# Weights laid out as one run per partition, and two loads held behind x, in a hybrid decoder layer on eight cores

## Chip, cores, metric

One Trainium2 chip, all 8 cores, one program on each. The time is the device time of the slowest core in microseconds (us). Most executions agree within 0.3%. Some fall into a slower state, in which the cores of one or both dies run longer; they are left out of every ratio.

## The reference, cut to what matters

One decoder layer on 8192 tokens of width 2048, causal, f32. Each core takes 1024 tokens and a halo of 128 (1152 columns, `TM`). All weights are read by every core.

```python
h = rms_norm(x, g_pre_mix) * (1.0 + scale_m) + shift_m     # mod = silu(c) @ w_ada + b_ada
u, v, p, ga, gb = split(h @ w_in)                          # 9216 columns
y_a = spatial_gating(gelu(u), gelu(v), ...) @ w_branch_a
y_b = multiscale_pool(p, ...) @ w_branch_b
mix = (sigmoid(ga) * y_a + sigmoid(gb) * y_b) @ w_out
x = x + gate_m * rms_norm(mix, g_post_mix)                 # "first/second norm pass" below
h = rms_norm(x, g_pre_ffn) * (1.0 + scale_f) + shift_f
a, g = split(causal_depthwise_conv(h @ w_up))
x = x + gate_f * rms_norm((gelu(a) * g) @ w_down, g_post_ffn)
```

## The kernel before

A small recording layer (`Sched`) collects every operation with what it reads and writes, orders the operations of each engine by a simulated clock, and puts in the semaphore waits. Hence one line of the source (L296, L303, L330 and so on) stands for all matmuls, all activations or all transfers; the tile names tell them apart. Activations lie feature-major (128 features on the partitions, tokens along the row). Weights are f32 in HBM and are cast to bf16 by the transfer, which GpSimd issues. They go to a ring of three slots (`RING`); x and the output are moved by transfers that SyncE issues.

```python
def load(key, where, w, r0, nk, c0, ncols, parts=1, only=None, after=()):
    dst = piece_dst(where, nk, ncols)
    n = nk // parts
    for i in range(parts) if only is None else only:
        d = dst[:, i * n:(i + 1) * n, :]
        src = w[(r0 + i * n) * 128:(r0 + (i + 1) * n) * 128, c0:c0 + ncols].rearrange("(k p) n -> p k n", p=128)
        last = S.dma("pool", d, src, writes=[d])
```

A slot is 16 k-blocks (kc) by 512 columns: each partition gets 16 separate rows of 512 f32, 2 KB read and 1 KB landed. Pieces of `w_ada` have rows of 1536 or 2048 columns (6 or 8 KB read), but for sB, whose rows are 512. Pieces are named after what they hold: sA, sB, h, gm, sf, hf, gf are parts of `w_ada`; pA, v, u of `w_in`; o of `w_out`; up of `w_up`. kc 12 to 15 are the last four k-blocks of the normalised x; they need sB's scale.

The start, cut: `sA0` to `sA3` and `sB` are the parts of `w_ada` that give the first scale (12 of 16 blocks of features from the sA, four from sB), `pA` the first projection weights (`w_in`, in four transfers of four kc).

```python
load("sA0", 0, *specs["sA0"]);  load("sA1", 1, *specs["sA1"])
for kc in range(KC):
    S.dma("sp", xres[kc], xT[kc * 128:(kc + 1) * 128, :], writes=[xres[kc]])
...
for kc in range(6): x_stats(kc)          # square on ScalarE, sum by a matmul with ones
scale_mms("sA0", 0, 0, 12)
load("sA2", 0, *specs["sA2"])
for kc in range(6, 12): x_stats(kc)
scale_mms("sA1", 4, 0, 12)
load("sA3", 1, *specs["sA3"])
load("pA", 2, *specs["pA"], only=[0, 1, 2])
...                                      # rstd, x * rstd, then sA2, sB, pA[3], sA3, scale, h for kc 0 to 11
```

The first norm pass (642 columns, `PCS_1`), which adds x again, stores the sum, and takes the next mean square, beside output-projection matmuls:

```python
for i in range(16):
    m, x = mixT[:, i, c0:c0 + n], xs[i % len(xs)]
    S.dma("sp", x, xT[i * 128:(i + 1) * 128, 126 + c0:126 + c0 + n], writes=[x])
    S.tt(m, m, rs, ALU.mult)
    S.tt(m, m, x, ALU.add)
    S.act(sqx[i % 4][:, 0:n], m, AF.Square)
    sum_mms(b0, sqx[i % 4], pieces, i == 0, i == 15)
    S.dma("sp", outT[...], mixT[:, i, lo:c0 + n], ...)
```

`up000` is the first piece of `w_up`; GpSimd issues it when the ring slot of `o1` is free, which falls into this pass.

Of the kernel before, what the change touches and what calls it, by code (L numbers as in the profile page):

```python
# [14 lines left out]
D = 2048  # L15
# [22 lines left out]
class Sched:  # L38
# [5 lines left out]

    def __init__(self):
        self.ops = []
        self.mem = {}
        self.tags = {}
        self.names = list(self.ENGS) + ["d%s%d" % (e, i) for e, n in self.NDMA.items() for i in range(n)]
        self.classes = {"pe": 0, "pes": 1, "act": 2, "dve": 3, "pool": 4, "dma": 5}  # L50
# [161 lines left out]

    def emit(self, block, sems):
        seq = self.order()
        self.prods = {p: [] for p in self.names}
        q = {e: [] for e in self.ENGS}
        know = {e: {} for e in self.ENGS}
        next_dma = {e: 0 for e in self.NDMA}
        for o in seq:
            deps = {}  # L220
            if o.dma:
                i = next_dma[o.eng]
                next_dma[o.eng] = (i + 1) % self.NDMA[o.eng]
                o.prod, o.inc = "d%s%d" % (o.eng, i), 16
            else:
                o.prod, o.inc = o.eng, 1
            o.seq, o.signal, o.waits = len(self.prods[o.prod]), o.dma, []
            if o.dma and o.seq:
                deps[o.prod] = o.seq - 1
            for d in o.deps:  # L230
                d = self.ops[d]
                if d.eng == "pe" and o.eng == "pe":
                    continue
                if deps.get(d.prod, -1) < d.seq:
                    deps[d.prod] = d.seq
            k = know[o.eng]
            todo = [(p, s) for p, s in deps.items() if k.get(p, -1) < s]
            for p, s in list(todo):
                if any(self.prods[p2][s2].know.get(p, -1) >= s for p2, s2 in todo if (p2, s2) != (p, s)):
                    todo.remove((p, s))  # L240
            for p, s in todo:
                d = self.prods[p][s]
                d.signal = True
                o.waits.append((p, s))
                for p2, s2 in d.know.items():
                    if k.get(p2, -1) < s2:
                        k[p2] = s2
                if k.get(p, -1) < s:
                    k[p] = s
            o.know = dict(k)  # L250
            self.prods[o.prod].append(o)
            q[o.eng].append(o)
        self.q = q
        value = {}
        for p, lst in self.prods.items():
            n, vals = 0, []
            for o in lst:
                if o.signal:
                    n += o.inc
                vals.append(n)  # L260
            value[p] = vals

        def run(name, e):
            for o in q[name]:
                for p, s in o.waits:
                    e.wait_ge(sems[p], value[p][s])
                ins = o.fn(e)
                if o.signal:
                    ins.then_inc(sems[o.prod], o.inc)
            if name == "sp":  # L270
                for p, lst in self.prods.items():
                    if lst and p.startswith("d"):
                        e.wait_ge(sems[p], value[p][-1])

        block.tensor(lambda e: run("pe", e))
        block.scalar(lambda e: run("act", e))
        block.vector(lambda e: run("dve", e))
        block.gpsimd(lambda e: run("pool", e))
        block.sync(lambda e: run("sp", e))
# [51 lines left out]
                       after=after)  # L331


def build_program():
    nc = bass.Bass("TRN2", target_bir_lowering=False)

    def din(name, shape, dt=F32):
        return nc.dram_tensor(name, list(shape), dt, kind="ExternalInput").ap()

    xT = din("xT", [D, TM])  # L340
    c_col = din("c_col", [128, KC])
    w_ada = din("w_ada", [D, 6 * D])
    b_ada_fm = din("b_ada_fm", [128, 96])
    vec_fm_d = din("vec_fm", [128, NV])
    bs_exp_d = din("bs_exp", [1, 1024])
# [2 lines left out]
    wpool_d = din("wpool", [128, 4 * 2 * 256])  # L348
    hmask_d = din("hmask", [128, 1])
    pfix_d = din("pfix", [128, 64])  # L350
    w_in = din("w_in", [D, 9216])
    w_ba = din("w_branch_a", [D, D])
    w_bb = din("w_branch_b", [1024, D])
    w_out = din("w_out", [D, D])
    w_up = din("w_up", [D, 2 * FFN])
    w_down = din("w_down", [FFN, D])
    outT = nc.dram_tensor("outT", [D, TOK], F32, kind="ExternalOutput").ap()

    S = Sched()
# [1 line left out]
    with contextlib.ExitStack() as es:  # L361
# [40 lines left out]

        slot_queue = {}
        loaded = {}

        def piece_dst(where, nk, ncols):
            if isinstance(where, int):
                return v3(RING[:, where * 8192:where * 8192 + nk * ncols], nk)
            return view(where[0], where[1], nk * ncols * 2, BF16, nk)

        def load(key, where, w, r0, nk, c0, ncols, parts=1, only=None, after=()):
            dst = piece_dst(where, nk, ncols)
            n = nk // parts
            for i in range(parts) if only is None else only:
                d = dst[:, i * n:(i + 1) * n, :]
                src = w[(r0 + i * n) * 128:(r0 + (i + 1) * n) * 128, c0:c0 + ncols].rearrange("(k p) n -> p k n", p=128)
                last = S.dma("pool", d, src, writes=[d])
            loaded[key] = dst
            return last

        specs = {}
# [6 lines left out]
        def load_next(slot):  # L428
            if slot_queue.get(slot):
                key = slot_queue[slot].pop(0)  # L430
                load(key, slot, *specs[key])

        def bank(b):
            return ps[:, b * 512:(b + 1) * 512]
# [64 lines left out]

        def sec_specs(name, sec):  # L500
            for i in range(4):
                specs["%s%d" % (name, i)] = (w_ada, i * 4, 4, sec * D, D)

        for nm, sec in (("gm", 2), ("sf", 4), ("hf", 3), ("gf", 5)):
            sec_specs(nm, sec)
        for i in range(4):
            specs["sA%d" % i] = (w_ada, i * 4, 4, D, 1536)
        specs["sB"] = (w_ada, 0, KC, D + 1536, 512, 4)
        for i in range(8):
            specs["h%d" % i] = (w_ada, i * 2, 2, 0, D)  # L510
        specs["pA"] = (w_in, 0, KC, 4096 + 512, 512, 4)
        specs["pB"] = (w_in, 0, KC, 4096, 512)
        specs["bb0"] = (w_bb, 0, 8, 0, 1024)
        specs["bb1"] = (w_bb, 0, 8, 1024, 1024)
        for g in range(4):
            specs["u%d" % g] = (w_in, 0, KC, g * 512, 512)
            specs["v%d" % g] = (w_in, 0, KC, 2048 + g * 512, 512, 1 if g else 4)
            specs["ga%d" % g] = (w_in, 0, KC, 5120 + g * 512, 512)
            specs["gb%d" % g] = (w_in, 0, KC, 7168 + g * 512, 512)
            specs["ba%d" % g] = (w_ba, 0, KC, g * 512, 512)  # L520
            specs["o%d" % g] = (w_out, 0, KC, g * 512, 512)
        UPP = ((0, 512), (512, 512), (1024, 384))
        for k in range(NG):
            for half in range(2):
                for i, (c0, n) in enumerate(UPP):
                    specs["up%d%d%d" % (k, half, i)] = (w_up, 0, KC, half * FFN + k * GB * 128 + c0, n)
            for q in range(4):
                specs["dn%d%d" % (k, q)] = (w_down, k * GB, GB, q * 512, 512)

        run = ["v0", "gm0", "v1", "gm1", "v2", "gm2", "v3", "gm3", "u0", "u1", "u2", "u3"]  # L530
        mods = ["sf0", "sf1", "sf2", "sf3", "hf0", "hf1", "hf2", "hf3"]
# [42 lines left out]
        S.memset(vsum[:], 0.0)  # L574
        S.memset(vstat[:], 0.0)
        for kc in range(KC):
            S.dma("sp", xres[kc], xT[kc * 128:(kc + 1) * 128, :], writes=[xres[kc]])
            if kc == 7:
                for t, d in ((bada, b_ada_fm), (vec, vec_fm_d)):
                    S.dma("sp", t[:], d[:, :], writes=[t[:]])  # L580
# [13 lines left out]
        for kc in range(6):  # L594
            x_stats(kc)
        scale_mms("sA0", 0, 0, 12)
        load("sA2", 0, *specs["sA2"])
        for kc in range(6, 12):
            x_stats(kc)
        scale_mms("sA1", 4, 0, 12)  # L600
        load("sA3", 1, *specs["sA3"])
        load("pA", 2, *specs["pA"], only=[0, 1, 2])
        for kc in range(12, 16):
            x_stats(kc)
# [256 lines left out]
        def norms(pieces, rs, xs, b0):  # L861
            c0, n = pieces[0][0], sum(m for _, m in pieces)
            lo = max(c0, 2)
            for i in range(16):
                m, x = mixT[:, i, c0:c0 + n], xs[i % len(xs)]
                S.dma("sp", x, xT[i * 128:(i + 1) * 128, 126 + c0:126 + c0 + n], writes=[x])
                S.tt(m, m, rs, ALU.mult)
                S.tt(m, m, x, ALU.add)
                S.act(sqx[i % 4][:, 0:n], m, AF.Square)
                sum_mms(b0, sqx[i % 4], pieces, i == 0, i == 15)  # L870
                S.dma("sp", outT[i * 128:(i + 1) * 128, lo - 2:c0 + n - 2], mixT[:, i, lo:c0 + n],
                      reads=[mixT[:, i, lo:c0 + n]], wtags=["o%d.%d" % (i, c0)])
            rms(b0, rs, pieces)
# [223 lines left out]
```

## Time and profile before

| | before |
|---|---|
| median of four runs | 1947.71 us (1946.21 to 1997.91, the last slow) |
| spans of the eight cores, profiled run | 1928.1 to 1945.9 us |
| TensorE busy, slowest core | 1826.0 of 1945.9 us |
| transfers issued by GpSimd | 143,152 packets, 178.8 MB landed |
| last x chunk used, by core | 66.8 to 68.2 us |

How to read it: in the row of digits each digit is the busy share of a 40th of the span in tenths. In a group "out<-in" names tiles. A chain is followed back from the last instruction, so a transfer in it is one that something waited for. The prediction shows the lines.

### The profile page before, as it was taken

How to read it: one execution, taken by the hardware profiler on the slowest of the kernel's cores; microseconds unless marked ns; L12 is line 12 of the kernel's file. 1: busy time of each engine (PE TensorE's matmuls, PEld its weight loads, DVE VectorE, ACT ScalarE, POOL GpSimd, SP SyncE). 2: the span in 40 equal slices, each digit the busy share in tenths (PEclk: the TensorE clock that was granted, in tenths of full speed). 3: DMA queues.
4: the chain of work that ended last, by engine and by line, in shares of the span. 5: the costliest groups of instructions: out<-in, count | busy, mean ns of one | idle time of the engine just before them, and what ended most of it. 6: DMA issues, size and time to landing. Idle time of an engine off the chain costs nothing.

```text
span 1945.9 us, 28368 instructions; the slowest of 8 cores (1928.1 to 1945.9 us)
## 1 busy us (share of the span) xinstructions
PE 1826.0 (94%) x12186; PEld 1130.6 (58%) x12186; DVE 653.6 (34%) x716; ACT 564.8 (29%) x741; POOL 105.0 (5%) x111
## 2 busy tenths in 40 slices
PE   1399899999999999999998999999999999999997
PEld 0155544566666666667565654666546664566676
DVE  0452300133121202120675441235423453234557
ACT  2322211511101001023677221343104430044365
POOL 0110100000000000000000000000000000000000
PEclk8599999999999999999999999999999999999998
DMA  9999869775496978691884656552754445665386
GB/s 204 189 137 145 151 97 135 112 106 87 62 152 95 141 114 132 96 180 19 222 167 93 114 90 101 83 82 50 114 90 76 77 74 90 105 101 78 59 198 209
DMA packets 172908, 225.05 MB, mean 116 GB/s; under 512 B 4208, under 2 KB 151920, under 8 KB 172784
## 3 DMA queue, kind: packets, MB, share of 16 engines
q0 software_dynamic: 143152, 178.79, 59.7%
q1 hardware_dynamic: 29632, 44.45, 7.2%
q8 instruction: 97, 1.59, 0.3%
q14 instruction: 27, 0.22, 0.0%
HBM read 385.23 MB, written 16.78 MB: 207 GB/s over the span
## 4 chain that ended last, share of the span: by engine, by line
PE 79%; DMA 13%; DVE 2%; SPq 2%; issue 2%; ACT 2%; POOL 0%; DVEq 0%; ACTq 0%; POOLq 0%
PE ps L296 79%; DMA RING<-w_ada 8%; SPq L330 2%; DVE R L307 2%; DMA RC<-xT 1%; DMA RING<-w_in 1%; DMA SC<-xT 1%; DMA RING<-w_up 1%; ACT SC L303 1%; ACT RD L303 0%; DVE SC L307 0%; DVE RC L307 0%; ACT L303 0%; DVE SC L319 0%; ACT R L303 0%
## 5 line engine op out<-in xcount | busy, mean ns | idle before, releaser
L296 PE MATMUL ps<-RD,RING 128*128 128x342 bf16 (+3 forms) x6912 | 1032.4, 310 | 21.1 <-ACT RD L303 11.3
L296 PEld LDWEIGHTS ps<-RD,RING 128*128 128x128 bf16 x6912 | 672.9, 98 | 371.2 <-issue 30.2
L296 PE MATMUL ps<-RC,RING 128*128 128x512 bf16 (+4 forms) x2160 | 382.9, 334 | 1.8 <-DVE R L307 1.2
L319 DVE SCALAR_TENSOR_TENSOR SC<-SC,vec 128x1024 f32<-128x1024 f32 (+2 forms) x198 | 230.2, 1166 | 337.5 <-ACT SC L303 328.0
L296 PEld LDWEIGHTS ps<-RC,RING 128*128 128x128 bf16 x2160 | 205.7, 98 | 166.1 <-issue 4.0
L303 ACT ACTIVATE SC<-ps 128x1026 f32<-128x1026 f32 (+3 forms) x123 | 116.6, 949 | 543.9 <-PE ps L296 535.0
L303 ACT ACTIVATE R<-ps 128x512 bf16<-128x512 f32 (+3 forms) x76 | 62.3, 823 | 450.7 <-PE ps L296 450.7
L296 PE MATMUL ps<-RING,RD 128*128 128x512 bf16 x576 | 127.2, 382 | 6.8 <-DMA RING<-w_in 5.7
L303 ACT ACTIVATE SC<-SC,vec 128x1024 f32<-128x1024 f32 (+2 forms) x99 | 113.0, 1144 | 7.6
L296 PE MATMUL ps<-R,RING 128*128 128x342 bf16 x768 | 114.4, 308 | 0.0
L307 DVE TENSOR_TENSOR R<-R,RC 128x1026 f32<-128x1026 f32 (+5 forms) x61 | 61.4, 1040 | 153.2 <-ACT R L303 81.5
L307 DVE TENSOR_TENSOR R<-ps,R 128x1024 f32<-128x1024 f32 (+3 forms) x96 | 65.0, 688 | 128.3 <-PE ps L296 128.3
L296 PEld LDWEIGHTS ps<-RING,RD 128*128 128x128 bf16 x576 | 56.2, 99 | 76.7 <-issue 11.2
L296 PEld LDWEIGHTS ps<-R,RING 128*128 128x128 bf16 x768 | 74.5, 98 | 39.1 <-issue 1.7
L307 DVE TENSOR_TENSOR SC<-ps,SC 128x1026 f32<-128x1026 f32 x16 | 19.6, 1227 | 194.4 <-PE ps L296 194.4
L303 ACT ACTIVATE RC<-SC 128x1024 bf16<-128x1024 f32 (+2 forms) x55 | 48.6, 885 | 102.1 <-DVE SC L319 101.8
L307 DVE TENSOR_TENSOR R<-R,SC 128x642 f32<-128x642 f32 (+2 forms) x58 | 40.3, 747 | 87.0 <-ACT SC L303 77.9
L303 ACT ACTIVATE R<-R 128x256 bf16<-128x256 f32 (+4 forms) x97 | 57.8, 604 | 36.0 <-DVE R L307 34.9
L330 POOL DMA_DIRECT2D RING<-w_up x24 | 27.4, 1142 | 579.2 <-PE ps L296 579.2
L296 PE MATMUL ps<-SC,RING 128*128 128x342 bf16 x384 | 57.2, 308 | 0.9 <-ACT RC L303 0.6
L307 DVE TENSOR_TENSOR RC<-RC,SC 128x1024 bf16<-128x1024 bf16 x44 | 53.9, 1225 | 4.6
L296 PE MATMUL ps<-RC,RD 128*128 128x321 bf16 (+3 forms) x368 | 51.2, 291 | 0.0
(93 smaller groups left out, 693.1 us busy)
## 6 DMA issues: line engine op xcount, KB each, us to landing
RING<-w_in POOLq DMA_DIRECT2D x16, 2048.0 KB, 26.6
RING<-w_ada POOLq DMA_DIRECT2D x16, 2048.0 KB, 17.5
RING<-w_up POOLq DMA_DIRECT2D x16, 2048.0 KB, 14.1
RING<-w_down POOLq DMA_DIRECT2D x15, 1408.0 KB, 10.8
RING<-w_up POOLq DMA_DIRECT2D x8, 1536.0 KB, 11.9
R<-xT SPq DMA_DIRECT2D x15, 576.0 KB, 33.8
RING<-w_ada POOLq DMA_DIRECT2D x8, 1024.0 KB, 23.1
RING<-w_branch_a POOLq DMA_DIRECT2D x4, 2048.0 KB, 15.6
```

The source lines that it names most:

```text
L296: return self.op("pe", lambda e: e.matmul(out, lhsT=lhsT, rhs=rhs, start=start, stop=stop), [lhsT, rhs], [out], side=side, cost=cost, lat= ...
L303: return self.op("act", lambda e: e.activation(out=out, in_=in_, func=func, bias=bias, scale=scale, accum_out=accum), self._aps(in_, scale ...
L307: return self.op(eng, lambda e: e.tensor_tensor(out=out, in0=in0, in1=in1, op=op), [in0, in1], [out], cost=65.0 + 1.05 * self._n(out))
L319: return self.op("dve", lambda e: e.scalar_tensor_tensor(out=out, in0=in0, scalar=s, in1=in1, op0=op0, op1=op1), self._aps(in0, s, in1), [ ...
L330: return self.op(eng, lambda e: e.dma_start(out=out, in_=in_), reads, writes, rtags, wtags, dma=True, cost=b / 300.0, after=after)
```

## The change

Intent: on the host, lay the weights out so that every piece that is loaded is one contiguous run per partition. That makes few, long packets (mostly 32 KB read, 16 KB landed; a packet in these profiles is one contiguous run). Two waits go with it: sA2 and sA3 are not issued before the last x chunk has landed, up000 not before the last x chunk of the first norm pass. `late` moves the held operation, and what follows it on its engine, behind the one it waits for.

```diff
+    for o, d in self.late:
+        i, j = seq.index(o), seq.index(d)
+        if i < j:
+            moved = [q for q in seq[i:j] if q.eng == o.eng]
+            seq[i:j + 1] = [q for q in seq[i:j + 1] if q.eng != o.eng] + moved
+        o.deps.append(d.id)
...
+def lay(name, w):
+    w = np.asarray(w, np.float32)
+    nk = w.shape[0] // 128
+    return np.concatenate([w[:, c:c + n].reshape(nk, 128, n).transpose(1, 0, 2).reshape(128, nk * n) for c, n in SPLITS[name]], axis=1)
...
-                d = dst[:, i * n:(i + 1) * n, :]
-                src = w[(r0 + i * n) * 128:(r0 + (i + 1) * n) * 128, c0:c0 + ncols].rearrange("(k p) n -> p k n", p=128)
-                last = S.dma("pool", d, src, writes=[d])
+                d = dst[:, i * n:(i + 1) * n]
+                last = S.dma("pool", d, wt[w][:, src0 + i * n:src0 + (i + 1) * n], writes=[d], after=after)
...
+                if key in hold:
+                    S.late.append((o, hold[key]))
...
-            S.dma("sp", xres[kc], xT[kc * 128:(kc + 1) * 128, :], writes=[xres[kc]])
+            last_x = S.dma("sp", xres[kc], x_l[:, kc * TM:(kc + 1) * TM], writes=[xres[kc]])
...
-        load("sA2", 0, *specs["sA2"])
+        S.late.append((load("sA2", 0, *specs["sA2"]), last_x))
...
-        load("sA3", 1, *specs["sA3"])
+        S.late.append((load("sA3", 1, *specs["sA3"]), last_x))
...
-                S.dma("sp", x, xT[i * 128:(i + 1) * 128, 126 + c0:126 + c0 + n], writes=[x])
+                hold["up000"] = S.dma("sp", x, x_l[:, i * TM + 126 + c0:i * TM + 126 + c0 + n], writes=[x])
```

(Cut: the tables of pieces, and the same layout for x and for each weight.)

More of the change, by code (lines that the diff above doesn't have):

```diff
@@ L46, in __init__ @@
         self.ops = []
+        self.late = []
         self.mem = {}
@@ L214, in emit @@
         seq = self.order()
+        for o, d in self.late:
[4 more added lines that the diff above has]
+            o.deps.append(d.id)
+        at = {o.id: i for i, o in enumerate(seq)}
+        assert all(at[d] < at[o.id] for o in seq for d in o.deps)
         self.prods = {p: [] for p in self.names}
@@ L331, in dma, with place @@
                        after=after)
+SPLITS = {
+    "w_ada": [(0, D), (D, 1536), (D + 1536, 512)] + [(s * D, D) for s in range(2, 6)],
+    "w_in": [(c, 512) for c in range(0, 9216, 512)],
+    "w_branch_a": [(c, 512) for c in range(0, D, 512)],
+    "w_branch_b": [(0, 1024), (1024, 1024)],
+    "w_out": [(c, 512) for c in range(0, D, 512)],
+    "w_up": [(h * FFN + k * GB * 128 + c, n) for k in range(NG) for h in range(2) for c, n in ((0, 512), (512, 512), (1024, 384))],
+    "w_down": [(c, 512) for c in range(0, D, 512)],
+}
+KBLOCKS = {"w_branch_b": 8, "w_down": 44}
+def place(name, c0):
+    nk, off = KBLOCKS.get(name, KC), 0
+    for c, n in SPLITS[name]:
+        if c == c0:
+            return off
+        off += nk * n
+    raise KeyError((name, c0))
+def lay(name, w):
+    w = np.asarray(w, np.float32)
+    nk = w.shape[0] // 128
+    return np.concatenate([w[:, c:c + n].reshape(nk, 128, n).transpose(1, 0, 2).reshape(128, nk * n) for c, n in SPLITS[name]], axis=1)
 def build_program():
@@ L338, in din @@
         return nc.dram_tensor(name, list(shape), dt, kind="ExternalInput").ap()
-    xT = din("xT", [D, TM])
+    x_l = din("x_l", [128, KC * TM])
     c_col = din("c_col", [128, KC])
-    w_ada = din("w_ada", [D, 6 * D])
     b_ada_fm = din("b_ada_fm", [128, 96])
@@ L350, in build_program @@
     pfix_d = din("pfix", [128, 64])
-    w_in = din("w_in", [D, 9216])
-    w_ba = din("w_branch_a", [D, D])
-    w_bb = din("w_branch_b", [1024, D])
-    w_out = din("w_out", [D, D])
-    w_up = din("w_up", [D, 2 * FFN])
-    w_down = din("w_down", [FFN, D])
+    wt = {n: din(n, [128, KBLOCKS.get(n, KC) * sum(m for _, m in sp)]) for n, sp in SPLITS.items()}
     outT = nc.dram_tensor("outT", [D, TOK], F32, kind="ExternalOutput").ap()
@@ L404, in build_program, with load @@
         loaded = {}
+        hold = {}
         def piece_dst(where, nk, ncols):
             if isinstance(where, int):
-                return v3(RING[:, where * 8192:where * 8192 + nk * ncols], nk)
-            return view(where[0], where[1], nk * ncols * 2, BF16, nk)
-        def load(key, where, w, r0, nk, c0, ncols, parts=1, only=None, after=()):
+                return RING[:, where * 8192:where * 8192 + nk * ncols]
+            return view(where[0], where[1], nk * ncols * 2, BF16)
+        def load(key, where, w, k0, nk, c0, ncols, parts=1, only=None, after=()):
             dst = piece_dst(where, nk, ncols)
-            n = nk // parts
+            n = nk // parts * ncols
+            src0 = place(w, c0) + k0 * ncols
             for i in range(parts) if only is None else only:
-                d = dst[:, i * n:(i + 1) * n, :]
-                src = w[(r0 + i * n) * 128:(r0 + (i + 1) * n) * 128, c0:c0 + ncols].rearrange("(k p) n -> p k n", p=128)
-                last = S.dma("pool", d, src, writes=[d])
-            loaded[key] = dst
+                d = dst[:, i * n:(i + 1) * n]
+                last = S.dma("pool", d, wt[w][:, src0 + i * n:src0 + (i + 1) * n], writes=[d], after=after)
+            loaded[key] = v3(dst, nk)
             return last
@@ L430, in load_next @@
                 key = slot_queue[slot].pop(0)
-                load(key, slot, *specs[key])
+                o = load(key, slot, *specs[key])
+                if key in hold:
+                    S.late.append((o, hold[key]))
         def bank(b):
@@ L501, in sec_specs @@
             for i in range(4):
-                specs["%s%d" % (name, i)] = (w_ada, i * 4, 4, sec * D, D)
+                specs["%s%d" % (name, i)] = ("w_ada", i * 4, 4, sec * D, D)
         for nm, sec in (("gm", 2), ("sf", 4), ("hf", 3), ("gf", 5)):
@@ L506, in build_program @@
         for i in range(4):
-            specs["sA%d" % i] = (w_ada, i * 4, 4, D, 1536)
-        specs["sB"] = (w_ada, 0, KC, D + 1536, 512, 4)
+            specs["sA%d" % i] = ("w_ada", i * 4, 4, D, 1536)
+        specs["sB"] = ("w_ada", 0, KC, D + 1536, 512, 4)
         for i in range(8):
-            specs["h%d" % i] = (w_ada, i * 2, 2, 0, D)
-        specs["pA"] = (w_in, 0, KC, 4096 + 512, 512, 4)
-        specs["pB"] = (w_in, 0, KC, 4096, 512)
-        specs["bb0"] = (w_bb, 0, 8, 0, 1024)
-        specs["bb1"] = (w_bb, 0, 8, 1024, 1024)
-        for g in range(4):
-            specs["u%d" % g] = (w_in, 0, KC, g * 512, 512)
-            specs["v%d" % g] = (w_in, 0, KC, 2048 + g * 512, 512, 1 if g else 4)
-            specs["ga%d" % g] = (w_in, 0, KC, 5120 + g * 512, 512)
-            specs["gb%d" % g] = (w_in, 0, KC, 7168 + g * 512, 512)
-            specs["ba%d" % g] = (w_ba, 0, KC, g * 512, 512)
-            specs["o%d" % g] = (w_out, 0, KC, g * 512, 512)
+            specs["h%d" % i] = ("w_ada", i * 2, 2, 0, D)
+        specs["pA"] = ("w_in", 0, KC, 4096 + 512, 512, 4)
+        specs["pB"] = ("w_in", 0, KC, 4096, 512)
+        specs["bb0"] = ("w_branch_b", 0, 8, 0, 1024)
+        specs["bb1"] = ("w_branch_b", 0, 8, 1024, 1024)
+        for g in range(4):
+            specs["u%d" % g] = ("w_in", 0, KC, g * 512, 512)
+            specs["v%d" % g] = ("w_in", 0, KC, 2048 + g * 512, 512, 1 if g else 4)
+            specs["ga%d" % g] = ("w_in", 0, KC, 5120 + g * 512, 512)
+            specs["gb%d" % g] = ("w_in", 0, KC, 7168 + g * 512, 512)
+            specs["ba%d" % g] = ("w_branch_a", 0, KC, g * 512, 512)
+            specs["o%d" % g] = ("w_out", 0, KC, g * 512, 512)
         UPP = ((0, 512), (512, 512), (1024, 384))
@@ L525, in build_program @@
                 for i, (c0, n) in enumerate(UPP):
-                    specs["up%d%d%d" % (k, half, i)] = (w_up, 0, KC, half * FFN + k * GB * 128 + c0, n)
+                    specs["up%d%d%d" % (k, half, i)] = ("w_up", 0, KC, half * FFN + k * GB * 128 + c0, n)
             for q in range(4):
-                specs["dn%d%d" % (k, q)] = (w_down, k * GB, GB, q * 512, 512)
+                specs["dn%d%d" % (k, q)] = ("w_down", k * GB, GB, q * 512, 512)
         run = ["v0", "gm0", "v1", "gm1", "v2", "gm2", "v3", "gm3", "u0", "u1", "u2", "u3"]
@@ L1069 @@
         "c_col": np.ascontiguousarray(fm(c[0], 16)),
-        "w_ada": np.ascontiguousarray(w_ada[0], f),
+        "w_ada": lay("w_ada", w_ada[0]),
         "b_ada_fm": np.ascontiguousarray(fm(b_ada[0], 96)),
@@ L1076 @@
         "wpool": np.ascontiguousarray(np.asarray(w_pool[0], f).reshape(4, 2, 128, 256).transpose(2, 0, 1, 3).reshape(128, 2048)),
-        "w_in": np.ascontiguousarray(w_in[0], f),
-        "w_branch_a": np.ascontiguousarray(w_branch_a[0], f),
-        "w_branch_b": np.ascontiguousarray(w_branch_b[0], f),
-        "w_out": np.ascontiguousarray(w_out[0], f),
-        "w_up": np.ascontiguousarray(w_up[0], f),
-        "w_down": np.ascontiguousarray(w_down[0], f),
+        "w_in": lay("w_in", w_in[0]),
+        "w_branch_a": lay("w_branch_a", w_branch_a[0]),
+        "w_branch_b": lay("w_branch_b", w_branch_b[0]),
+        "w_out": lay("w_out", w_out[0]),
+        "w_up": lay("w_up", w_up[0]),
+        "w_down": lay("w_down", w_down[0]),
     }
@@ L1086 @@
         m = dict(common)
-        m["xT"] = np.ascontiguousarray(xpad[core * TOK:core * TOK + TM].T)
+        m["x_l"] = np.ascontiguousarray(xpad[core * TOK:core * TOK + TM].T.reshape(KC, 128, TM).transpose(1, 0, 2).reshape(128, KC * TM))
         m["pfix"] = _pool_fix(core == 0)
```

## The prediction

> **What bounds the kernel now.** I read the page first, for where TensorE is not busy.
>
> ```profile
> PE 1826.0 (94%) x12186; PEld 1130.6 (58%) x12186; DVE 653.6 (34%) x716; ACT 564.8 (29%) x741; POOL 105.0 (5%) x111
> PE   1399899999999999999998999999999999999997
> DMA  9999869775496978691884656552754445665386
> q0 software_dynamic: 143152, 178.79, 59.7%
> ```
>
> TensorE works 1826 of 1946 us; no change to loads can shorten those 1826 us, so at most 120 us are at stake, most of them in the first two slices (48.6 us each). The next view is the busy time by stretch (engine, busy us, then granted clock, DMA share, GB/s landed).
>
> ```profile
> 0.00:93.20 93.20, 21.51 (x240) 10.87 (x241) 20.46 (x28) 24.98 (x23) 9.25 (x16) 0.70 0.97 199
> 110.00:240.00 130.00, 118.02 (x810) 73.17 (x809) 55.77 (x59) 28.99 (x29) 12.53 (x16) 0.99 0.95 149
> 930.00:1050.00 120.00, 109.59 (x696) 67.13 (x694) 81.93 (x137) 87.67 (x142) 3.42 (x3) 0.97 0.74 176
> 1050.00:1850.00 800.00, 797.17 (x4952) 477.15 (x4951) 309.17 (x258) 230.43 (x222) 43.57 (x41) 1.00 0.55 87
> ```
>
> The idle sits in the start (93.2 - 21.5 = 72 us), in 110 to 240 us (12), around the change of sub-layer (10.4) and, in a stretch not shown, in the tail (13). The FFN's 800 us lose 3 us although their weights stream the whole time: those loads are hidden. Then TensorE's waits (total us, times, longest):
>
> ```profile
> PE ps L296 <- DMA RING<-w_ada: 46.4, 10, 27.8
> PE ps L296 <- ACT SC L303: 29.7, 16, 10.8
> PE ps L296 <- ACT RD L303: 13.3, 4, 10.4
> PE ps L296 <- DMA RING<-w_in: 5.7, 1, 5.7
> ```
>
> Of the 46.4, 27.8 is the first matmul and 10.4 the fourth scale block (sA3); the ACT SC waits are squares of x that wait for x chunks. Both are the start's DMA. The chain, in order of time (start, us), names the transfers on the path:
>
> ```profile
> 38.38 28.83 DMA RC<-xT
> 67.34 1.17 ACT SC L303
> ...
> 91.82 1.26 ACT RD L303
> ...
> 948.26 13.72 DMA SC<-xT
> ```
>
> The last x chunk lands at 67.2; 26 us of statistics and normalising follow, to the first projection matmul at 93.2. Last, POOL's order of time and the DMA views of three stretches (40 to 60, 70 to 102, and 1192 to 1199 us):
>
> ```profile
> 64.16 0.74 POOL L330 DMA_DIRECT2D RING<-w_ada  x1 [33.65 <-PE ps L296]
> ```
> ```profile
> DMA packets 1449, 5.09 MB, mean 254 GB/s; under 512 B 134, under 2 KB 224, under 8 KB 1449
> ```
> ```profile
> DMA packets 4211, 4.98 MB, mean 156 GB/s; under 512 B 124, under 2 KB 3832, under 8 KB 4209
> ```
> ```profile
> DMA packets 1408, 1.44 MB, mean 206 GB/s; under 512 B 0, under 2 KB 1408, under 8 KB 1408
> ```
>
> Weight loads read f32 and land bf16, so what they read is twice what they land: 2 x 156 = 312 GB/s in the start, 2 x 206 = 412 GB/s in a quiet moment later, both with 2 KB runs (1 KB landed). The same descriptors that give 312 can give 412: in the start their size is not the limit.
>
> **What the Trainium skill says.** "HBM Reference", Specifications (TRN2): two cores share a domain, about 358 GB/s each when both stream, about 425 alone. The trace fits: 312 at the start, where all cores load, 412 later. "DMA: Bandwidth & Descriptors", "Why small descriptors are slow (HBM only)": a fixed cost per packet that matters at 256 B and below. Taken over the trace's packet records, the median of a 1,024-byte packet is 98 ns, of 2,048 173, of 4,096 324: some 22 ns fixed, 75 ns per KB. But w_ada's 4,096-byte packets land no faster while the HBM is shared (means of 390 to 450 ns between 250 and 930 us). Same page, "Queues, rings and completion order": an engine alternates between queues at packet granularity; longer weight packets would then push x and store packets aside. No run shows that yet. Same page, "Latency and other measured facts": row pitches of 2 MiB and more slow copies, 512 KiB hardly. The new per-partition pitches work out at 64 to 768 KiB; no run shows them.
>
> **The change part by part.** TensorE, VectorE and ScalarE instructions and their order stay identical (I compared the built programs). SyncE keeps its order. GpSimd keeps its order of loads and gains two waits.
>
> 1. Weights are laid out on the host so that a partition's whole piece is one run: 24 to 32 KB read instead of 4 to 16 rows of 2 to 8 KB. Bytes are unchanged. The per-packet saving applies only where the engine is the limit (at most 412 to about 435 GB/s, 16 x 2,048 B / 75 ns), and there the loads are hidden. Where HBM is shared I allow 3%. x gets the same treatment, but its 4,608-byte rows stay 4,608 bytes: worth nothing.
>
> 2. The loads sA2 and sA3 are issued only when the last x chunk has landed. Before x is complete the queues now carry sA0, sA1 (6.3 MB read), x (9.4) and 0.3 of constants: 16.0 MB at about 315 GB/s after 4 us of start = 55 us, against 67.2 now, when sA2's 3.1 MB share the way. The first projection matmul then comes at 55 + 26 = 81. But that is not where the start ends: kc 12 to 15 need sB and the last piece of pA, and in the old trace that piece landed at 108.1 (issued 81.79, 26.3 to landing) and those matmuls began at 108.7. The bytes up to there are the same 30.7 MB. The old order loses some 4 us of transfer at 62 to 70, because sA3 (64.16) waits for TensorE; the new one loses some 3 between x's end and sA2's first byte. So at the same rate the end moves from 108 to about 107; at 3% more, to about 104. TensorE, done with its first 72 matmuls (12.5 us) at 94, only waits longer there. Gain 1 + 3 = 4 us.
>
> 3. up000 waits for the last x chunk of the first norm pass. Now it is issued at 949.26, one us after that chunk (948.26), which then takes 13.7 us against a median of 8.2 for these sixteen. Without it, about 6 us sooner; TensorE loses only 0.87 + 2.47 + 0.67 us behind that chain at 962 to 991, so the gain is 3 us. up000 then starts at about 955 and, at 300 GB/s for 4.2 MB plus 2 us, lands at about 971, before its first matmul at 976.5.
>
> 4. The other DMA waits: v0 5.7; h0 and gm1 to gm3 1.1 + 1.5 + 1.9 + 1.0; w_up 1.2: 12.4 us. Each ends 14 to 26 us after its issue, so 3% is 0.4 to 0.8 us from each: 3 us.
>
> Sum 4 + 3 + 3 = 10 us: 1947.7 - 10 = 1937.
>
> **The rivals.** (a) Long runs read HBM better than 2 KB runs while two cores share it: 10% more rate. For: 312 is under the skill's 358. Against: the 8 KB runs of w_ada show no gain. The start then gains about 10 (TensorE's own 81 + 12.5 + sB's matmuls and normalising cap it near 98), the waits 8, norms 3: 1926. (b) The new pitches or the long packets slow the reads by 5%: start +5, waits +6, norms -3: about 1955. (c) Long weight packets starve x: x would land late after up000's successors or beside sA0 and sA1. Against: sA0 and sA1 end anyway before x does, so x's end is set by the byte sum; the second norm pass's x is issued at 976 to 986 and first added after 1008. I expect 0 to 3 us. (d) The early x saves the full 12 us: it would if sB did not bind; 1929.
>
> **Range and chances.** The size hangs on the shared rate: 1926 at +10%, 1937 at +3%, 1943 at none, 1955 at -5%. Range 1921 to 1951. Over 2% faster needs 39 us, a third of all TensorE's idle time: 0.05. Over 2% slower needs 39 us more, a loss of some 15 to 20% in rate: 0.03.
>
> **What would show it.** Step 1: read rate at 70 to 102 us near 320, with far fewer packets. Step 2: last x lands near 54, first projection matmul near 80, a wait for w_ada (sB) of 5 us or more ahead of kc 12, whose matmuls start at 103 to 107. Step 3: the last x chunk before 962 takes 6 to 8 us and TensorE's waits at 962 to 991 shrink. Step 4: waits of 4 us for w_in and 0.5 to 1.5 for w_ada. I am wrong if the shared rate leaves 305 to 340, if sB lands well before 100, or if TensorE's busy time changes by over 5 us.

## The result

The changed kernel takes 1935.44 us (median of 10 runs, 1933.67 to 1938.84), the kernel before 1947.46 (median of 15 runs, three of them slow). The ratio is 0.9948, 95% interval 0.9938 to 0.9957. A ratio here is the mean time of one kernel's fast runs over that of the other's in the same rounds, so not quite the ratio of the medians. The forecast was 1937, with a range of 1921 to 1951.

The page of the changed kernel, its parts 1 to 3 (the lines that answer to those of before):

```profile
PE 1827.5 (95%) x12186; PEld 1130.5 (58%) x12186; DVE 652.1 (34%) x716; ACT 566.2 (29%) x741; POOL 57.7 (3%) x111
PE   2489899999999999999999999999999999999997
DMA  9898866744475756690874455333443334544276
q0 software_dynamic: 15408, 178.79, 50.3%
```

TensorE's work is unchanged (1826.0 and 1827.5 us). The same bytes go in 15,408 packets instead of 143,152, and GpSimd's busy time, most of it issuing transfers, fell from 105.0 to 57.7 us. Busy time by stretch, as before:

```profile
0.00:93.20 93.20, 28.95 (x269) 13.67 (x270) 24.53 (x32) 31.23 (x28) 6.69 (x16) 1.00 0.92 194
110.00:240.00 130.00, 120.92 (x819) 74.09 (x818) 55.51 (x59) 28.90 (x28) 7.58 (x14) 0.97 0.89 148
930.00:1050.00 120.00, 111.78 (x714) 69.23 (x713) 80.08 (x137) 89.96 (x146) 2.11 (x4) 0.97 0.70 175
```

The first column after the length is TensorE: its idle time shrank from 71.7 to 64.3 us in the first stretch, by 2.9 us in the second, by 2.2 us in the third (the slowest core is core 1 before and core 4 after; the table of landmarks below compares like with like). TensorE's waits and the chain in order of time:

```profile
PE ps L305 <- DMA RING<-w_ada: 49.1, 8, 20.3
PE ps L305 <- ACT SC L312: 25.3, 20, 9.7
PE ps L305 <- ACT RD L312: 4.2, 3, 3.1
PE ps L305 <- DMA RING<-w_in: 3.9, 1, 3.9
```
```profile
37.34 19.31 DMA RC<-x_l
57.18 15.26 DMA RING<-w_ada
75.24 30.09 DMA RING<-w_ada
...
939.67 9.45 DMA SC<-x_l
949.65 18.25 DMA RING<-w_up
```

The wait for w_ada did not shrink, it moved: the first matmul comes at 20.3 instead of 27.8 us, but TensorE now waits for sA2, sA3 and sB. In the chain the last x chunk lands at 56.7 (67.2 before), and in its place stand sA2 and then sB (75.24 + 30.09 = 105.3). In the norm pass the last x chunk takes 9.45 us (13.72 before), and the next link is new: the held up000.

The order of instructions on TensorE is the same in all kernels, so the start of the n-th matmul can be compared between traces. Over the six cores whose records are complete in both, the changed kernel is ahead by this much:

| Landmark (n-th matmul) | before, us | after, us | ahead by | gained on the way |
|---|---|---|---|---|
| first projection matmul (240) | 92.9 | 84.0 | 8.9 | 8.9 |
| ninth matmul of kc 12 to 15 (384) | 110.3 | 106.8 | 3.5 | -5.4 |
| after h1 (600) | 144.9 | 139.9 | 5.1 | 1.6 |
| first v stage, past its wait (1250) | 252.7 | 244.5 | 8.2 | 3.2 |
| before the norm pass (5000) | 811.9 | 803.0 | 9.0 | 0.8 |
| first up blocks (6100) | 979.5 | 968.2 | 11.2 | 2.3 |
| second up blocks (6600) and end | 1061.9 | 1049.9 | 12.0 | 0.8 |

These six cores gained 12.0 us on average, all eight 11.1; the metric, the slowest core, 0.52% or 10.1 us.

The granted TensorE clock differs as well: its mean over a core is 0.977 to 0.981 before and 0.984 to 0.995 in the changed kernel (0.70 and 1.00 in the first stretch). That is not where the time comes from: the layout alone (below) has 0.990 to 0.997 and is slower than the kernel before.

### The profile page after: what moved, and what is told of

It is laid out like the page before. It is cut to its first block, busy times and chain, and to the rows that moved or that the text cites. A ratio compares the mean times of both kernels' runs of the same rounds, so it can differ in the third digit from the quotient of the medians.

```text
span 1933.5 us, 28370 instructions; the slowest of 8 cores (1917.2 to 1933.5 us)
## 1 busy us (share of the span) xinstructions
PE 1827.5 (95%) x12186; PEld 1130.5 (58%) x12186; DVE 652.1 (34%) x716; ACT 566.2 (29%) x741; POOL 57.7 (3%) x111
## 3 DMA queue, kind: packets, MB, share of 16 engines
q0 software_dynamic: 15408, 178.79, 50.3%
## 4 chain that ended last, share of the span: by engine, by line
PE 85%; DMA 9%; SPq 2%; DVE 1%; issue 1%; ACT 1%; POOL 0%; DVEq 0%; ACTq 0%; POOLq 0%
PE ps L305 85%; DMA RING<-w_ada 5%; SPq L339 2%; DMA RING<-w_in 1%; DMA RC<-x_l 1%; DMA RING<-w_up 1%; DMA SC<-x_l 1%; DVE R L316 1%; ACT SC L312 1%; ACT RD L312 0%; DVE RC L316 0%; DVE SC L328 0%; DVE SC L316 0%; POOL RING L339 0%; ACT L312 0%
## 5 line engine op out<-in xcount | busy, mean ns | idle before, releaser
L305 PE MATMUL ps<-scb,RING 128*128 128x1 bf16 x256 | 7.9, 165 | 46.7 <-DMA RING<-w_ada 46.7
## 6 DMA issues: line engine op xcount, KB each, us to landing
RING<-w_up POOLq DMA_DIRECT2D x8, 1536.0 KB, 11.3
```

Source lines behind the costliest of these rows:

```text
L305: return self.op("pe", lambda e: e.matmul(out, lhsT=lhsT, rhs=rhs, start=start, stop=stop), [lhsT, rhs], [out], side=side, cost=cost, lat= ...
```

## The experiments

Eleven runs were made (ten new kernels, and the changed one again), all correct, each timed in five rounds against the kernel before. "Ahead" below is the same comparison of landmarks, over all eight cores: it uses the n-th weight load of TensorE, whose records are complete on every core and which starts within 0.3 us of the n-th matmul. These are one profile each. "All fast runs" is the mean span of the eight cores over all fast runs, against the kernel before in the same rounds.

### The four combinations: layout and holds

The layout without the holds:

```diff
-        S.late.append((load("sA2", 0, *specs["sA2"]), last_x))
+        load("sA2", 0, *specs["sA2"])
         (the same for sA3)
-                hold["up000"] = S.dma("sp", x, x_l[...], writes=[x])
+                S.dma("sp", x, x_l[...], writes=[x])
```

> The new layout without either hold (order and waits of before). The change as a whole took 12.0 us off (mean of six cores): 5.1 up to the first blocks of mixer B, 3.2 at the first v matmul, 0.7 at gm1 to gm3, 2.3 at the first norm pass, 0.7 at w_up. Theory A (prediction): the layout gives about 3 us of the start and the waits for v0, gm and w_up (4.5), the norm pass gives nothing back: 6 to 8 us faster, ratio 0.996 to 0.997, last x chunk of the start at 64 to 67 us. Theory B: the layout does all, the holds nothing: 11 to 12 us faster, 0.994. Theory C: long weight packets push x aside and the holds only repair that: last x chunk of the start later than 67.2 us, last x chunk of the norm pass over 14 us, total no faster than before, 1.000 or above.

The holds without the layout (the same lines put into the kernel before):

> The old layout with both holds. Theory A: x lands near 55 us, the first projection matmul near 82, but kc 12 starts at 107 to 110 as before, start gain 1 us; norm pass gain 2 to 3; other waits unchanged: 3 to 4 us faster, ratio 0.998. Theory B: nothing, ratio 1.000. Theory D (the early x is what shortens the start, the layout gives only the later waits): start gain 5, norm pass 2.3: 7 us faster, 0.996.

The layout with the hold of sA2 and sA3 alone:

> The change without the hold of up000. Theory A: start as in the changed kernel (5 us), v0, gm, w_up as well, but the norm pass gives nothing: last x chunk of the first norm pass 13 us or more to landing, total 9 to 10 us faster, 0.995. Theory C: the x chunk is starved by 12 to 16 KB packets (over 17 us to landing) and the norm pass is 3 us or more slower than before: 6 us faster, 0.997.

The layout with the hold of up000 alone:

> The change without the holds of sA2 and sA3. Theory A: start gain 3 us rather than 5, rest as in the changed kernel: 9 to 10 us faster, 0.995. Theory D: start gain 0, 7 us faster, 0.9965. Theory C: start slower than before by 3 us or more, 4 us faster, 0.998.

Measured (ahead of before in us; minus is behind):

| | kc 12 (384) | v stage (1250) | before norms (5000) | gained in the norm pass (5000 to 6100) | end, mean core | all fast runs, mean core | ratio [95%] |
|---|---|---|---|---|---|---|---|
| layout alone | -0.2 | 4.6 | 5.2 | -8.3 | -2.5 | -4.2 | 1.0023 [1.0011, 1.0035] |
| holds alone | -3.5 | -1.9 | -1.7 | 0.8 | -0.7 | 0.6 | 1.0000 [0.9988, 1.0012] |
| layout + hold of sA | 2.7 | 7.9 | 8.8 | -7.6 | 1.9 | -2.1 | 1.0013 [0.9999, 1.0026] |
| layout + hold of up000 | 0.3 | 4.8 | 5.0 | 2.0 | 7.8 | 7.3 | 0.9952 [0.9934, 0.9969] |
| all (the change) | 3.1 | 7.7 | 8.5 | 1.9 | 11.1 | 9.7 | 0.9948 [0.9938, 0.9957] |

Half of the runs of the fourth kernel (2118 to 2277 us) are left out; its fast runs are 1935.1 to 1938.3.

Neither half is worth anything alone. The layout alone is slower, the holds alone do nothing, and together they save half a per cent. Most of that hangs on one wait: with the new layout, holding up000 turns 1.0023 into 0.9952. Theory C was right for the norm pass and wrong for the start, where the layout alone did no harm. The chain of the layout with the hold of sA alone shows the harm (slowest core, start and length):

```profile
926.01 7.72 DMA SC<-x_l
...
937.02 23.48 DMA SC<-x_l
```

The last x chunk of the norm pass takes 23.48 us, against 13.72 before and 9.45 with the hold. It is not so on every core: in the profile of the layout alone the stretch from matmul 5800 to 6100 takes 65 to 67 us on six of the eight cores and 49 to 51 on the other two (52 to 56 before). What decides which cores escape was not settled: up000 is issued 1.7 to 1.8 us after the last x chunk on the two that escape and on two that don't.

The holds alone put kc 12 back by 3.5 us, where I had expected a gain of 1. Their chain:

```profile
58.62 27.61 DMA RING<-w_ada
86.76 26.36 DMA RING<-w_in
```

x comes nearly as early as in the changed kernel (last chunk used at 57.0 to 59.0 us by core, against 55.0 to 57.3), but the loads that must follow it, sA2 to the last piece of pA, end at 113.1 in the old layout.

That does not dispose of theory D, that x sets the start. Set side by side (means of the eight cores, us), the four kernels show two paths that end together ahead of kc 12:

| | last x lands | first projection matmul | last piece of pA lands | ninth matmul of kc 12 to 15 |
|---|---|---|---|---|
| before | 67.1 | 92.8 | 107.1 | 110.3 |
| layout alone | 66.9 | 92.9 | 100.5 | 110.5 |
| holds alone | 57.7 | 90.8 | 111.6 | 113.8 |
| both | 56.0 | 84.7 | 104.9 | 107.2 |

The layout alone ends the loads 6.6 us sooner, and kc 12 does not move: the path from x, through normalising and TensorE's own matmuls, takes as long as before. The start of its chain has x and no load ahead of kc 12:

```profile
47.59 19.13 DMA RC<-x_l
78.32 11.50 DVE R L316 x9
92.74 14.79 PE ps L305 x136
```

In the kernel before it is the same, closely: from 95 to 112 us TensorE has one wait on every core, 1.6 us for normalising (slowest core below), and none for a load.

```profile
108.69 5.40 PE L296 MATMUL ps<-RD,RING 128*128 128x347 bf16 x24 [1.61 <-DVE RD L313]
```

The first matmul of kc 12 starts 0.6 to 4.5 us after the last piece of pA there, 6 to 12 us after it with the layout alone, but 0.25 us after it, on every core, with the holds alone and with both: there the loads are the bound. The holds alone bring x 9.4 us sooner and put the loads 4.5 us later. Only both halves shorten both paths, which is why neither gains at kc 12 by itself.

### Where the bytes lie, or how long a packet is

New layout, no holds, but each row followed by 256 bytes that are not read, so that a row is its own run again:

```diff
-        off += nk * n
+        off += nk * (n + PAD)                      # PAD = 64
...
-  S.dma("pool", d, wt[w][:, src0 + i * n:src0 + (i + 1) * n], writes=[d], after=after)
+  S.dma("pool", v3(d, m), v3(wt[w][:, src0 + i * m * (ncols + PAD):src0 + (i + 1) * m * (ncols + PAD)], m)[:, :, 0:ncols], ...)
```

> The layout of the change, but every row of a block followed by 256 bytes of padding, so that the packets land 1 KB (w_in, w_up and others) to 4 KB (w_ada) again; no holds. It tells where the bytes lie from how long a packet is. Theory A (packet length does both: fewer packets end loads sooner, long packets keep x back): as the kernel before: last x chunk of the norm pass 11 to 14 us to landing, first v matmul no more than 2 us sooner than before, over 140,000 packets, ratio 1.000. Theory B (the new addresses do it): first v matmul 5 to 8 us sooner than before as in the layout-only run, and the x chunk 20 to 24 us.

The ratio is 1.0004 (0.9990 to 1.0018), the queue's line is that of before:

```profile
q0 software_dynamic: 143152, 178.79, 60.0%
```

The v stage is 0.7 us ahead (4.6 in the layout-only run) and the last x chunk takes 10.76 us on the slowest core. The bytes lie almost where the new layout puts them, and the gain at the v stage and the harm in the norm pass are gone. So both come from the length of the packets, as theory A says. Two things stay open. The padding also changes the pitch per partition (68 to 800 KiB instead of 64 to 768), so what the exact new pitches do is not shown. And in the start the last piece of pA lands at 102.8 here (107.1 before, 100.5 with long packets), which packet length does not explain; kc 12 hardly moves (0.5 us).

How much a load gains can be read from loads that have no other near them (32 loads of w_branch_a over the eight cores, mean from issue to the last packet's end): 14.66 us before, 13.14 with long packets, 14.77 with padded rows. Of the 1.5 us, 0.4 is an earlier first packet (1.82 to 1.42 us after the issue began; GpSimd issues 2,048 runs in 1.15 us and 128 in 0.53) and 1.1 a shorter transfer (12.84 to 11.72 us, 9%). For w_ada, whose rows were 4 KB landed already, it is 13.04 to 12.69.

### How x is pushed aside

First, an in-between length: up000 to up002 in four transfers each, so that packets land 4 KB, without the hold of up000.

```diff
-  specs["up%d%d%d" % (k, half, i)] = ("w_up", 0, KC, half * FFN + k * GB * 128 + c0, n)
+  specs["up%d%d%d" % (k, half, i)] = ("w_up", 0, KC, half * FFN + k * GB * 128 + c0, n, 4 if k + half == 0 else 1)
```

> Without the hold of up000, but up000 to up002 in four transfers each, so that their packets land 4 KB instead of 16 KB (with the hold of sA2 and sA3, to be compared with that run, 1.0013, last x chunk 20 to 24 us on most cores). Theory A1 (an engine takes one packet of each queue in turn): up000 has 32 packets per engine of 324 ns; the x and store packets queued ahead of the last chunk are some 70 per engine (8.5 us at about 320 GB/s), so all of up000 still goes first, 10 us: 18 to 22 us to landing, ratio 1.000 to 1.001. Theory A2 (delay in proportion to packet length): 13 to 15 us, as with 1 KB, ratio 0.996 to 0.997.

The ratio is 1.0024 (1.0010 to 1.0037). The last x chunk but one on the slowest core, which is the one in its chain:

```profile
936.00 21.11 DMA SC<-x_l
```

The last chunk takes 20.4 to 24.1 us, on all eight cores now. Packets a quarter as long delay x as much: theory A1 (the DMA engine takes one packet of each queue in turn) held, delay in proportion to length (A2) did not. (One thing else differs from the run it is compared with: the first quarter of up000 is issued 0.6 to 2.6 us ahead of the last x chunk, not 1 to 2 us behind it.) The arithmetic is the number of turns. Up000 has 128 packets of 1 KB per engine before, 32 of 4 KB, or 8 of 16 KB; the 70 or so packets of x and stores that stand ahead of the last chunk (an estimate from 8.5 us at 320 GB/s over 16 engines) outnumber the 32 and the 8, so all of up000 goes through first.

The packet records show the turns. While both queues have work, the weight packets and the packets of x and stores start in nearly equal numbers, whatever their lengths: 532 and 520 in the kernel before (1 KB, 954 to 962 us), 97 and 89 with the hold of sA alone (16 KB, core 5, 944 to 955 us), 179 and 175 in the run with x chunk 8 below (12 KB, core 3, 52 to 68 us). The x and store packets are 2.5 to 4.6 KB. Counts can't tell one packet in turn from a few in turn.

Second, the release of up000 by x chunk 12 of the pass instead of 15, in the changed kernel:

```diff
+                if i <= 12:
+                    hold["up000"] = xd                # xd: the x load of block i
```

> The changed kernel with up000 released by x chunk 12 of the first norm pass instead of chunk 15. In the changed kernel six of eight cores then wait for up000 (18 to 20 us from issue to landing). Theory A: the last chunks queue behind up000 for most of its 10 us again: 15 us or more to landing, norm pass no faster, 0 to 6 us slower than the changed kernel: 0.995 to 0.998. Rival (up000 is the bound and three chunks are little): up to 3 us faster than the changed kernel, 0.9935.

The ratio is 0.9974 (0.9960 to 0.9988), slower than the change. The slowest core's last x chunk:

```profile
939.95 19.17 DMA SC<-x_l
```

Three chunks are enough to be caught, though not on every core: the last chunk takes 25 and 19 us on two cores, 13 on two, and 7 to 9 on four. Theory A held for the time, the rival fell.

Third, in the start: sA2 and sA3 released by x chunk 8 instead of 15.

```diff
-            last_x = S.dma("sp", xres[kc], x_l[...])
+            o = S.dma("sp", xres[kc], x_l[...])
+            if kc == 8:
+                last_x = o
```

> The changed kernel with sA2 and sA3 released by x chunk 8. Theory A (the sum of bytes up to kc 12 sets the end of the start, as long as x + 26 + 12.5 us is earlier): x lands 2 to 5 us later than in the changed kernel, the first projection matmul too, yet kc 12 starts within 2 us of the release by chunk 12 (103.2 us, mean of six cores) and the time is within 2 us of that run: 0.992 to 0.9935. Theory D (the landing of x sets it): 3 to 5 us slower than the changed kernel, 0.9965.

The ratio is 1.0030 (1.0018 to 1.0042); I expected 0.992 to 0.9935. ScalarE squares each x chunk as it lands. These are the squares around the release, slowest core, in order of time (start, length, and the idle time before with what ended it):

```profile
46.81 1.16 ACT L312 ACTIVATE SC<-R 128x1152 bf16<-128x1152 f32 x1 [0.93 <-DMA R<-x_l]
49.09 1.16 ACT L312 ACTIVATE SC<-R 128x1152 bf16<-128x1152 f32 x1 [1.12 <-DMA R<-x_l]
59.78 1.16 ACT L312 ACTIVATE SC<-R 128x1152 bf16<-128x1152 f32 x1 [9.54 <-DMA R<-x_l]
71.00 1.16 ACT L312 ACTIVATE SC<-R 128x1152 bf16<-128x1152 f32 x1 [10.05 <-DMA R<-x_l]
75.99 1.16 ACT L312 ACTIVATE SC<-R 128x1152 bf16<-128x1152 f32 x1 [3.83 <-DMA R<-x_l]
81.95 1.16 ACT L312 ACTIVATE SC<-RC 128x1152 bf16<-128x1152 f32 x1 [4.79 <-DMA RC<-x_l]
```

Chunks come every 2 us, then, once sA2 flows, every 11, and later every 5 to 6. A chunk is 8 packets per engine. In this trace's packet records one packet of sA2 or sA3 lands 12 KB and takes 1.14 us on average (50 to 72 us), an x packet beside it 0.28, so eight turns of both are 11.3 us; one of pA lands 4 KB and takes 0.37 us, x then 0.23, eight turns 4.8 us. That is the turn by turn account, with sizes that fit. x ends at 82 instead of 56, and the first projection matmul comes 26 us after x, at 107.3 (mean of eight cores; 84.7 in the changed kernel): here x sets the start. My expectation had kept the sum of bytes and forgotten the turns, although the runs of the norm pass had shown them by then.

### A version that beats both

sA2 and sA3 released by x chunk 12: late enough that x is nearly through, early enough that the queues don't run dry (edit as above, with 12).

> The changed kernel with sA2 and sA3 released by x chunk 12 instead of 15, so that the DMA queues don't run dry between the last x and sA2 (about 3 us in the changed kernel at 56 to 59). Theory A (the byte sum up to kc 12 sets the end of the start): kc 12 and mixer B 2 to 3 us sooner than in the changed kernel, part of it lost again at v0; 1 to 3 us faster than it, 0.9935 to 0.9945 of before. Theory D (x landing sets it): x later by 1 to 3 us and so all later, 0.9955 or more.

The ratio is 0.9923 (0.9909 to 0.9936), 1931.78 us. The stretch from 57 to 60 us on core 4, first the changed kernel, then this one; the last two columns are the DMA share and GB/s landed:

```profile
57.00:60.00 3.00, 1.12 (x3) 0.29 (x3) 0.00 (x0) 1.66 (x2) 2.64 (x5) 1.00 0.13 20
```
```profile
57.00:60.00 3.00, 1.12 (x3) 0.29 (x3) 0.00 (x0) 1.64 (x3) 0.00 (x0) 1.00 1.09 172
```

The hole of 3 us is filled, kc 12 is 7.4 us ahead of before (3.1 in the changed kernel), the end 14.2 us (11.1). On one core x was already caught a little (its last square at 62.0 us instead of 56 to 59; 64.5 on one core of the next run, with the same release), so chunk 12 is close to the edge.

The same with up000 in four transfers of four kc, all still held:

```diff
-  ..., half * FFN + k * GB * 128 + c0, n)
+  ..., half * FFN + k * GB * 128 + c0, n, 1 if k + half + i else 4)
```

> The changed kernel with sA2 and sA3 released by x chunk 12 and up000 in four transfers of four kc each, all still held until the last x chunk of the first norm pass. Theory A: the 18 to 20 us from release to landing of up000 are the bound there; its first quarter lands after about 5 us and TensorE can start, but the last quarter lands when the whole did: 1 to 3 us faster than with the early release alone (0.9923), 0.991 to 0.992. Rival (the norm pass itself, VectorE and ScalarE, is the bound): no difference, 0.9923.

The ratio is 0.9923 (0.9911 to 0.9936): no better. The new wait for up000 did go: TensorE has it on five of eight cores with the early release alone (2.2 to 3.7 us), on none here, and the norm pass gained 3.8 us instead of 1.1. But between matmuls 6400 and 6600 it lost 2 us again. TensorE's waits in 925 to 1070 us on core 4, before this edit and with it:

```profile
PE ps L305 <- ACT SC L312: 3.4, 3, 2.1
```
```profile
PE ps L305 <- ACT SC L312: 5.0, 4, 3.3
```

TensorE came earlier and stood waiting for ScalarE's evictions behind the second norm pass; all its waits in this stretch add to 8.4 and 8.6 us. That this pass is the bound there is argued from these waits; no run took it away.

The changed kernel once more, on the chip of the last run and of the one with x chunk 8 (the other runs were on another chip):

> The changed kernel again, on the chip of the two runs beside it: 0.994 to 0.9955 of before. It shows how far the other two are from it without the difference between chips.

0.9936 (0.9924 to 0.9949), 1933.25 us, against 0.9923 for the version with the early release and the split of up000: the intervals overlap. That the early release (with the split) gains some 3 us is clear in the landmarks of each profile and in the mean core of all fast runs (1922.2 us against 1925.3), less so in the time of the slowest core.

## Why the prediction was right, point by point

- **Range and sum.** 1937 was forecast, 1935.44 measured. 10 us were forecast; 10.1 came by the ratio, 9.7 on the mean core of all fast runs, 11.1 in the profile. That the sum fits is partly luck, for it adds gains that do not add: the forecast for the layout alone was 6 to 8 us faster, and its mean core is 4.2 us slower; for the holds alone 3 to 4 us, and it is 0.6.
- **Step 1, 3% more rate.** The number came, the cause is not shown. The DMA view of the changed kernel at 70 to 102 us:

```profile
DMA packets 1103, 5.14 MB, mean 161 GB/s; under 512 B 128, under 2 KB 128, under 8 KB 964
```

  161 GB/s landed against 156, so 322 GB/s read against 312. But with the holds alone, in the old layout, the same stretch has 160 to 162 on every core (159 to 163 in the changed kernel, 151 to 157 before): this view measures what is in flight then, not the length of the packets. Loads that stand alone gained more, 9% of the transfer for 1 KB packets, 0.4 us from the issue besides.
- **Step 2, the start.** x at 55 (last chunk used at 55.0 to 57.3), kc 12 at 104 to 107 (the ninth matmul at 106.8, so the first near 105.6), a gap of 3 us behind x: as forecast. The first projection matmul came at 84 and not at 81, because sA3 lands later than the normalising ends, and the wait for w_ada ahead of kc 12 is 2.0 to 4.4 us by core, not 5 or more. What the step had wrong is the bound of the kernel before. It read the last piece of pA (108.1, kc 12 at 108.7) as what ends the start; no core waits for a load there, the path from x ends it, and that piece lands 0.6 to 4.5 us ahead of kc 12. The split was wrong with it: I gave the hold 1 us and the layout 3, added up. Alone the layout gave nothing at kc 12 and the holds took 3.5 away; only together they gave 3.1.
- **Step 3, the norm pass.** Forecast 3, measured 1.9; the last x chunk takes 6.5 to 9.4 us by core (forecast 6 to 8). up000 became the next wait, at 949.65 + 18.25 = 967.9 on the slowest core; I had it landing at 971 and not waited for. But the step told half of what the hold does. In the old layout the norm pass gained 0.8 with the holds. In the new one the hold is worth 9.5 (1.9 with it, -7.6 without), and 11.5 on the mean core of all fast runs (7.3 with it, -4.2 without, both without the hold of sA).
- **Step 4, other waits.** Forecast 3, measured 4.7 on the six cores of the first table: 3.15 at the v stage, 0.75 up to the norms, 0.77 at the second up blocks. It is not the even 0.4 to 0.8 us from each wait that the step had: most of it is one wait. (The 1.6 us gained between matmuls 384 and 600 are not assigned.)
- **Rival (c), long packets starve x.** The term that was mis-sized: "0 to 3 us" is right for the kernel as it was built, because its two holds keep the long packets away from x. Where the hold of up000 is missing the norm pass loses about 8 us on the mean core. I read the two waits as small gains; the one of up000 is the price of the layout.
- **Rivals (b) and (d).** No loss shows in the padded run, whose pitches are near the new ones. The early x was 8.9 us at the first projection matmul and 3.5 at kc 12: in the changed kernel the loads do bind, as the byte sum said, but with the new layout and without the hold of sA it is x that binds.

## What to carry to other kernels

In these runs longer packets ended a load a little sooner (13.14 against 14.66 us), but the DMA engines served two busy queues about one packet each in turn (97 and 89, 532 and 520), so a queue with long packets took the engine from a queue with short ones; count turns (packets per DMA engine), not bytes, to see how long a short-packet transfer is held up. When a change has two halves, run the four combinations before saying what each is worth: here each alone gave nothing, in the start because two paths ended within 5 us of each other and each half shortened one. Where one wait holds a large load back, try its release at several points: in the start x chunk 12, just before the queues ran dry, gave 0.9923, chunk 15 0.9948, and chunk 8, a few chunks too early, 1.0030, more lost than the whole change had won.

## What the Trainium skill lacked or had wrong

- "DMA: Bandwidth & Descriptors", Queues, rings and completion order, states the turn by packets, and the runs agree (179 weight packets to 175 of x). It lacks what that costs when packets differ in length: an x chunk of 8 packets per engine took 2 us alone, 5 to 6 beside 4 KB packets, 11 beside 12 KB packets.
- The same page, SWDGE vs HWDGE vs iDMA, gives a packet as "≤4096 B preferably". The records of these runs, whose packet is one contiguous run, have single packets of 12,288 and 16,384 landed bytes (24 and 32 KB read), with a median of 1,227 ns for the latter.
- The same page, Rules for kernel authors, advises to coalesce small transfers. Most of these loads were 1 to 2 MB (landed) before and after; the page has no word that fewer, longer runs within a load can hold up another queue. Here the layout alone was 0.23% slower (1.0023).
- The same page, Anatomy of one DMA, calls descriptor generation "small, variable" and gives no time for it. Issuing a 2 MB load (landed) took GpSimd 1.15 us with 2,048 runs and 0.53 us with 128.
